# Two-layer hybrid token mixer on one core: where the attention keys of the first head, and the Fourier weights, are put and who loads them

## The chip, the core and the metric

The kernel runs on one core of a Trainium2 chip. The metric is the time of one execution on the device in microseconds. Each kernel is run several times; the median of the runs is the time that counts. A profiled execution gives the trace, whose times count from the start of its span.

## What is computed

Two layers work on 2048 latent tokens and 256 context tokens of width 1024, all in float32. Each layer normalises its input, projects it, sends the parts to four branches, multiplies each by a gate and projects the whole back:

```python
h  = _rmsnorm(x, g) * (1 + scale) + shift
hp = h @ w_in                                   # 1024 -> q, kv, rope, conv, fourier, sgu, gate
attn = _block_attention(q, k_all, v_all)        # 4 heads, 64 + 32 (rope) deep, 2304 keys
conv = _conv_module(hp[..., CONV_OFF:FOUR_OFF], p)
mixed = jnp.fft.fft2(fg, axes=(1, 3), norm="ortho").real      # over tokens and 64 channels
four = mixed @ p["w_fourier"] + p["b_fourier"]
sgu  = _spatial_gating(hp[..., SGU_OFF:GATE_OFF], p)
y = concatenate([attn, conv, four, sgu]) * silu(hp[..., GATE_OFF:]) @ p["w_out"]
x = x + gate * y
```

The context stream goes through the same in the first layer; in the second only its keys and values are needed. The attention's softmax is over all 2304 keys.

## The kernel before

**Tiling.** Tokens and channels are cut into tiles of 128 partitions. Every float32 matmul of weight is written as three matmuls on halves of higher and lower bits (`mm3`, lines 286 to 288): high by high, high by low, low by high. ScalarE rounds a tile to its high half (`split`, L277), VectorE subtracts to get the low half (L278).

**Projection ("phase A").** Per layer, three superblocks of up to 768 tokens are projected. The weights come in blocks of 256 to 384 columns, each by four loads `wst<-winA/B/C` on SyncE's queue into two staging buffers `wst` (`load_w`, L467), and are split into a ring that holds seven loads of a 256-column weight. In the third superblock the weights come in the order f (Fourier input), c0, c1 (convolution) and so on. After the first weight, the Fourier branch is started (`fourier`); its steps are put between the projection's matmuls. It loads its weights `wf` on GpSimd's queue (L805) into a tile `fst` of the Fourier pool, loads its input `fx` back from memory on SyncE's queue (L812), multiplies wf by a cosine matrix on TensorE (L824), and folds fx on GpSimd and VectorE; the folded halves fh, fl and the products wch, wcl are multiplied in a PSUM bank `hold`. Its results go out as `four<-fx` (L925) and `four<-fb` (L961) on SyncE's queue.

**Attention.** After phase A its pool is closed and a pool `K0` is opened at the same addresses. Head 0's and head 1's keys, `k0h`, `k0l`, `k1h`, `k1l`, are 96 rows by 2304 tokens, loaded in three pieces of 512, 768 and 1024 tokens, each by two loads (64 rows of `kh`, 32 rope rows of `krh`). Query tiles `qh`, `ql` cover 256 tokens by three loads each. Then come `v` and the convolution's blocks `cac` (L1464), all of them stored by phase A in memory before. A job is 256 queries for two heads; a tile of 128 queries of one head has four score banks of 512 keys and one of 256. VectorE takes maxima over the banks (L1005), and ScalarE takes exponentials of all five (`e<-s`, L1014) after the last. TensorE transposes them (L1035) and multiplies by v (L1028). The second job in layer 0 is the context's (T), which has one bank of 256 keys per tile. The convolution's tail goes beside: cac is transposed on TensorE (L1484), normalised on VectorE to yn, and transposed back (L1495). A first job may use eight PSUM banks (s five, t two, o one).

**Order and waits.** A scheduler sets each engine's order of instructions; an engine's queue is worked off in order. A tile at an address waits for the last use of the tiles that lay there before. In the pool of phase A the addresses run: `wst`, `m`, the layer's tiles (`uk`, `uq`, `ws`, `bs`), `junk`, `sq`, and then the ring, whose pool lies behind. Head 0's keys, at the front of `K0` behind the q tiles, thus lie over tiles of which `wst` and the ring are used until the last projection; head 1's lie over the ring too.

Who loads: q of the first job for both heads and head 0's keys on GpSimd's queue, head 1's keys, q of the second job, v and cac on SyncE's.

## Time and profile before

| | us |
|---|---|
| median of three runs | 2961.28 |
| lowest, highest | 2960.53, 2970.81 |
| profiled execution | 2965.82 |
| its span | 2963.8 |
| TensorE busy | 2829.0 |
| VectorE busy | 1956.1 |
| ScalarE busy | 1206.9 |
| GpSimd busy | 569.2 |

The profiled execution has 2.0 us outside its span. An engine's busy time leaves out DMA issues. A time line lists instructions with their start, length and, in brackets, the idle time ahead with what ended it. The view of waits adds these idle times up. A view of windows gives each engine's busy time in a stretch, and the clock that was granted to TensorE as a share of full speed: 0.5 is its lower level of 1.2 GHz, 1.0 the upper of 2.4 GHz. A list of DMA issues gives sizes and the median time from issue to landing.

### The profile page before, as it was taken

The numbers are of one execution on the slowest core, as the hardware profiler recorded it, in microseconds if no ns is written. First come the engines' busy times: TensorE is split into PE (matmuls) and PEld (weight loads), VectorE is DVE, ScalarE is ACT, GpSimd is POOL, SyncE is SP. The second block draws the span as 40 slices with busy tenths as digits, with TensorE's granted clock in tenths as the row PEclk, the third lists the DMA queues.
The fourth block names the chain that finished last, engine by engine and source line by source line (L and its number), as shares of the span: only waits on it lengthen the run. The fifth ranks groups of instructions, "written<-read, shape, count | busy, mean of one in ns | idle before, by whom it ended". The sixth has DMA issues, their size and how long they took to land. (4 is left out here: it accounts for less than half of the span.)

```text
span 2963.8 us, 50552 instructions
## 1 busy us (share of the span) xinstructions
PE 2829.0 (95%) x18434; PEld 2429.3 (82%) x18434; DVE 1956.1 (66%) x4301; ACT 1206.9 (41%) x3228; POOL 569.2 (19%) x951
## 2 busy tenths in 40 slices
PE   6999999999699999999999999999979999999998
PEld 4889999899567777769998899998767777776998
DVE  5578488485377777654553695894827777775554
ACT  3432343433344454543322343343425455554432
POOL 2301311421211111112322212113321110011210
PEclk8999999999799999999999999999989999999999
DMA  7465343433521010016543443444453101000653
GB/s 244 139 194 177 107 132 106 161 123 117 163 56 29 29 48 25 21 30 207 182 153 117 157 158 105 137 136 139 148 164 93 33 22 45 18 28 15 187 155 110
DMA packets 221849, 326.75 MB, mean 110 GB/s; under 512 B 33456, under 2 KB 152752, under 8 KB 220832
## 3 DMA queue, kind: packets, MB, share of 16 engines
q1 hardware_dynamic: 191392, 240.66, 26.9%
q0 software_dynamic: 29776, 82.83, 8.3%
q8 instruction: 145, 2.38, 0.3%
q14 instruction: 104, 0.85, 0.1%
q10 hardware_dynamic: 432, 0.04, 0.0%
HBM read 232.30 MB, written 91.10 MB: 109 GB/s over the span
## 5 line engine op out<-in xcount | busy, mean ns | idle before, releaser
L1005 DVE TENSOR_REDUCE st<-s 128x1 f32<-128x512 f32 (+1 forms) x636 | 384.9, 631 | 184.4 <-PE s L288 182.6
L1014 ACT ACTIVATE e<-s,st 128x512 f32<-128x512 f32 (+1 forms) x636 | 399.4, 646 | 236.9 <-DVE st L1009 228.3
L286 PE MATMUL mm<-hh,ring 128*128 128x384 f32 (+1 forms) x1408 | 491.4, 349 | 0.0
L287 PE MATMUL mm<-hl,ring 128*128 128x384 f32 (+1 forms) x1408 | 484.7, 344 | 0.0
L288 PE MATMUL mm<-hh,ring 128*128 128x384 f32 (+1 forms) x1408 | 484.1, 344 | 0.0
L1451 DVE SCALAR_TENSOR_TENSOR acc<-win,c_cw,acc 128x384 f32<-128x384 f32 (+5 forms) x780 | 428.4, 572 | 7.4
L1035 PE MATMUL t<-ident,e 128*128 128x128 f32 x2320 | 341.8, 278 | 3.5 <-DVE et L1038 1.9
L1028 PE MATMUL o<-et,v 128*64 128x256 f32 x2320 | 343.7, 392 | 0.0
L1035 PEld LDWEIGHTS t<-ident,e 128*128 128x128 f32 x2320 | 259.7, 141 | 94.9 <-issue 43.7
L1038 DVE COPY et<-t 128x512 f32<-128x512 f32 x377 | 257.9, 686 | 92.1 <-PE t L1035 86.1
L286 PE MATMUL mm<-yh,woh 128*128 128x256 f32 x1040 | 297.2, 286 | 5.2 <-DVE xn L1223 3.7
L288 PE MATMUL mm<-yh,wol 128*128 128x256 f32 x1040 | 293.9, 283 | 0.2 <-DVE wol L278 0.2
L287 PE MATMUL mm<-yl,woh 128*128 128x256 f32 x1040 | 293.8, 282 | 0.1
L286 PEld LDWEIGHTS mm<-hh,ring 128*128 128x128 f32 x1408 | 267.8, 190 | 19.4 <-issue 9.5
L277 ACT CAST ring<-wst 128x256 fp32r<-128x256 f32 (+2 forms) x480 | 184.1, 418 | 240.2 <-DMA wst<-winC 125.4
L287 PEld LDWEIGHTS mm<-hl,ring 128*128 128x128 f32 x1408 | 267.9, 190 | 5.9
L288 PEld LDWEIGHTS mm<-hh,ring 128*128 128x128 f32 x1408 | 267.3, 190 | 5.8
L278 DVE TENSOR_TENSOR ring<-wst,ring 128x256 fp32r<-128x256 f32 (+2 forms) x480 | 201.2, 451 | 74.6 <-ACT ring L277 60.1
L1040 ACT COPY et<-t 128x512 f32<-128x512 f32 x203 | 119.1, 588 | 317.8 <-PE t L1035 317.6
L1028 PEld LDWEIGHTS o<-et,v 128*64 128x64 f32 x2320 | 153.1, 136 | 99.0 <-issue 51.9
L286 PEld LDWEIGHTS mm<-yh,woh 128*128 128x128 f32 x1040 | 198.4, 191 | 6.9 <-DVE xn L1223 4.3
L287 PEld LDWEIGHTS mm<-yl,woh 128*128 128x128 f32 x1040 | 198.3, 191 | 0.4 <-DVE yl L278 0.4
(319 smaller groups left out, 5284.8 us busy)
## 6 DMA issues: line engine op xcount, KB each, us to landing
wst<-winC SPq DMA_DIRECT2D x192, 256.0 KB, 3.1
ast<-wada SPq DMA_DIRECT2D x32, 512.0 KB, 4.5
gt<-g SPq DMA_DIRECT2D x102, 128.0 KB, 3.0
g<-co POOLq DMA_DIRECT2D x60, 192.0 KB, 2.2
wst<-winB SPq DMA_DIRECT2D x24, 384.0 KB, 3.4
x<-xn POOLq DMA_DIRECT2D x72, 128.0 KB, 2.8
ast<-wada SPq DMA_DIRECT2D x8, 1024.0 KB, 9.6
fst<-ft SPq DMA_DIRECT2D x32, 256.0 KB, 3.2
```

What stands on the lines that cost most here:

```text
L277: a = self.nc.scalar.copy(out=hi, in_=src)
L278: b = self.nc.vector.tensor_tensor(lo, src, hi.bitcast(F32), op=ALU.subtract)
L286: mm(out, lhsT=lh, rhs=rh, start=start and i == 0, stop=False)
L287: mm(out, lhsT=lh, rhs=rl, start=False, stop=False)
L288: self.last = mm(out, lhsT=ll, rhs=rh, start=False, stop=stop and i == n - 1)
L1005: self.red = nc.vector.reduce_max(mx[:, i:i + 1], ps[:, :w], axis=AX.X)
L1014: nc.scalar.activation(out=e, in_=ps, func=AF.Exp, bias=nb[:, 0:1], accum_out=sm[:, i:i + 1])
L1028: nc.tensor.matmul(job.o[64 * q:64 * q + 64, 0:256], lhsT=vt[:, g, 64 * h:64 * h + 64], rhs=et[:, 256 * q:256 * q + 256], start=kt == 0, s ...
L1035: nc.tensor.transpose(ps[:, j * P:(j + 1) * P], job.es[j][kt], self.ident)
L1038: nc.vector.tensor_copy(et, ps)
L1040: nc.scalar.copy(out=et, in_=ps)
L1451: eng.scalar_tensor_tensor(ac, win[:, t:t + w], v["cw"][:, l, c, t:t + 1], ac, op0=ALU.mult, op1=ALU.add)
```

## The change

`phase_a_open` now takes the layer's tiles, `m`, `sq` and `junk` from the pool before the first staging tile, so that these lie in front and `wst` behind them, next to the ring. `K0` takes head 0's keys first, then q, then head 1's keys: head 0's keys and the first q now lie over the layer's tiles, `m`, `sq` and `junk`, and no longer over `wst` and the ring; head 1's keys lie over `wst` and the ring.

All loads of the first two jobs go on SyncE's queue in the order of their use: q of head 0, keys of head 0, q of head 1, keys of head 1, q of the second job, v. The Fourier weights go through a staging tile `wst`, loaded on SyncE's queue right after the weight f, and are read from there by TensorE; their tile in the Fourier pool is gone. The number of loads is the same.

```diff
     def phase_a_open(self, l, lp):
 
+        self.sp = lp
+        self.ltiles = self.layer_tiles(lp)
+        self.m = [self.t(lp, f"m{c}", [P, SBW]) for c in range(2)]
+        self.sq(), self.junk()
         self.ringx = self.pool(f"ring{l}", "left")
...
                 if ci == 0 and i == 2:
+                    wf = self.t(lp, "wst", [P, 768], bufs=2)[:, :512].rearrange("p (a b) -> p a b", b=256)
+                    self.nc.sync.dma_start(out=wf, in_=A["wf"][l])
                     while self.dq:
                         self.tick()
...
-        wf = T_("fst", [P, 512], bufs=2).rearrange("p (a b) -> p a b", b=256)
-        nc.gpsimd.dma_start(out=wf, in_=A["wf"][l])
...
+    def load_k(self, S, kk, h):
+
+        for a, b in ((0, 512), (512, 1280), (1280, NTOK)):
+            s = slice(a, b)
+            for part, k in zip("hl", kk):
+                self.nc.sync.dma_start(out=k[0:64, s].bitcast(F32), in_=S["k" + part][64 * h:64 * h + 64, s])
+                self.nc.sync.dma_start(out=k[64:96, s].bitcast(F32), in_=S["kr" + part][:, s])
...
-                    q0 = [self.load_q(S, k0p, q, 0, nc.gpsimd) for q in range(2)]
-                    keys = self.load_k(S, k0p, 0)
-                    q1 = [self.load_q(S, k0p, q, 256 if last else T, nc.sync) for q in range(2)]
+
+                    keys = [[self.t(k0p, f"k0{part}", [96, NTOK], F32R) for part in "hl"]]
+                    q0 = [self.load_q(S, k0p, 0, 0)]
+                    self.load_k(S, keys[0], 0)
+                    q0.append(self.load_q(S, k0p, 1, 0))
+                    keys.append([self.t(k0p, f"k1{part}", [96, NTOK], F32R) for part in "hl"])
+                    self.load_k(S, keys[1], 1)
+                    q1 = [self.load_q(S, k0p, q, 256 if last else T) for q in range(2)]
                     nc.sync.dma_start(out=vt, in_=S["v"][:, :, :])
```

The order of instructions shows where this lands. SyncE's queue at the end of phase A in layer 0, before; a name ahead of the arrow is the tile written, behind it the source, and the brackets hold what the instruction waits for (PE is TensorE, DMAHW a load on SyncE's own queue, DMASW one on GpSimd's):

```order
L961 DMA four_110<-fb_7604 128x256 [waits DVE_49]
L961 DMA four_110<-fb_7672 128x256 [waits DMAHW6_49,DVE_49]
L975 DMA k1h_7829<-kh_94 64x512 [waits DMAHW7_49,PE_49,Activation_49]
L976 DMA k1h_7829<-krh_98 32x512 [waits DMAHW0_49]
L975 DMA k1l_7830<-kl_95 64x512 [waits DMAHW1_49]
```

The same place in the changed kernel:

```order
L963 DMA four_110<-fb_7606 128x256 [waits DVE_49]
L963 DMA four_110<-fb_7674 128x256 [waits DMAHW7_49,DVE_49]
L988 DMA qh_7803<-qh_96 64x256 [waits DMAHW0_49]
L991 DMA qh_7803<-qrh_100 16x256 [waits DMAHW1_49]
...
L972 DMA k0h_7801<-kh_94 64x512 [waits DMAHW6_49]
L973 DMA k0h_7801<-krh_98 32x512 [waits DMAHW7_49]
...
L991 DMA ql_7827<-qrl_101 16x256 [waits DMAHW7_49]
L972 DMA k1h_7831<-kh_94 64x512 [waits DMAHW0_49,PE_49,Activation_49]
```

The wait for TensorE stood ahead of the first key load; now 24 loads stand ahead of it.

SyncE's queue in the third superblock of layer 1, before, from the second load of c0 to the Fourier input (`fst<-ft` are the Fourier tables):

```order
L467 DMA wst_22810<-winC 128x512 [waits DMAHW3_49,DMAHW1_49,DVE_49]
L467 DMA wst_22816<-winC 128x512 [waits DMAHW2_49,DVE_49]
L467 DMA wst_22822<-winC 128x512 [waits DMAHW3_49,DVE_49]
L467 DMA wst_22971<-winC 128x512 [waits DMAHW4_49,DVE_49,Activation_49]
L467 DMA wst_22977<-winC 128x512 [waits DMAHW5_49,DVE_49]
L467 DMA wst_22983<-winC 128x512 [waits DMAHW6_49,DVE_49]
L467 DMA wst_22989<-winC 128x512 [waits DMAHW7_49,DVE_49]
L467 DMA wst_23136<-winC 128x512 [waits DMAHW0_49,DVE_49]
L812 DMA fx_22861<-f_17362 128x2048 [waits DMASW2_49,DMASW4_49,DMASW1_49,PE_49]
```

The same place in the changed kernel, from the Fourier weights on:

```order
L776 DMA wst_22794<-wf 128x512 [waits DMAHW1_49,DVE_49]
L467 DMA wst_22810<-winC 128x512 [waits DMAHW4_49,DMAHW2_49,DVE_49]
L467 DMA wst_22816<-winC 128x512 [waits DMAHW4_49,DVE_49]
L467 DMA wst_22822<-winC 128x512 [waits DMAHW5_49,DVE_49]
L467 DMA wst_22828<-winC 128x512 [waits DMAHW6_49,DVE_49]
L467 DMA wst_22975<-winC 128x512 [waits DMAHW7_49,DVE_49]
L467 DMA wst_22981<-winC 128x512 [waits DMAHW0_49,DVE_49]
L814 DMA fx_22865<-f_17364 128x2048 [waits DMASW3_49,DMASW1_49,PE_49]
L860 DMA fst_22965<-ft 128x512 [waits DMAHW3_49,PE_49]
L467 DMA wst_22987<-winC 128x512 [waits PE_49]
```

The four loads of c0 and two of c1 now pass through the one buffer that wf leaves free; the third of c1 waits for TensorE's last use of wf.

TensorE in layer 0, from the last scores of the first job to the first cac, before:

```order
L288 MATMUL s_8013<-k1h_7829,ql_7811 128x256
L286 MATMUL s_8076<-k0h_7815,qh_7843 128x256 [waits DMAHW4_49,DMAHW5_49,DMAHW3_49,Activation_49]
L287 MATMUL s_8076<-k0l_7816,qh_7843 128x256
L288 MATMUL s_8076<-k0h_7815,ql_7847 128x256 [waits DMAHW7_49,DMAHW6_49,DMAHW0_49]
L1484 MATMUL t_8092<-ident,cac_7872 128x128 [waits DMAHW0_49,Activation_49]
```

And in the changed kernel (the twelve matmuls of the T job's four tiles, of which the first and the last are shown):

```order
L288 MATMUL s_8015<-k1h_7831,ql_7827 128x256
L286 MATMUL s_8078<-k0h_7801,qh_7845 128x256 [waits DMAHW5_49,DMAHW6_49,DMAHW4_49,Activation_49]
...
L286 MATMUL s_8182<-k1h_7831,qh_7853 128x256 [waits Activation_49]
L287 MATMUL s_8182<-k1l_7832,qh_7853 128x256
L288 MATMUL s_8182<-k1h_7831,ql_7857 128x256
L1492 MATMUL t_8094<-ident,cac_7874 128x128 [waits DMAHW1_49]
```

One T tile's scores stood ahead of cac; now all four do.

## Rows read from the trace of the kernel before

**Rows 1.** Busy time of TensorE, share of the span and instructions (page, part 1).

```profile
PE 2829.0 (95%) x18434; PEld 2429.3 (82%) x18434; DVE 1956.1 (66%) x4301; ACT 1206.9 (41%) x3228; POOL 569.2 (19%) x951
```

**Rows 2.** TensorE's waits: us in total, times, longest in us.

```profile
PE s L286 <- DMA k0l<-krl: 27.5, 2, 14.1
...
PE hold L824 <- DMA fst<-wf: 10.8, 2, 6.3
...
PE mm L286 <- ACT ring L277: 4.6, 2, 3.8
...
PE hold L286 <- ACT fh L277: 1.9, 1, 1.9
```

**Rows 3.** Time line, TensorE, attention's start in layer 0: start, length, instruction, idle before.

```profile
764.21 0.77 PE L286 MATMUL s<-k0h,qh 96*128 96x512 f32 x1 [13.47 <-DMA k0l<-krl]
...
792.14 0.40 PE L288 MATMUL s<-k1h,ql 96*128 96x512 f32 x1
792.38 0.28 PE L286 MATMUL s<-k1h,qh 96*128 96x256 f32 x1
...
792.62 0.28 PE L288 MATMUL s<-k1h,ql 96*128 96x256 f32 x1
...
793.57 0.44 PE L1484 MATMUL t<-ident,cac 128*128 128x128 f32 x2
...
796.97 0.41 PE L1495 MATMUL t<-ident,yn 128*128 128x128 f32 x2 [0.32 <-DVE yn L1491]
```

**Rows 4.** Time line, TensorE, attention's start in layer 1.

```profile
2207.99 0.77 PE L286 MATMUL s<-k0h,qh 96*128 96x512 f32 x1 [14.05 <-DMA k0l<-krl]
...
2230.89 0.38 PE L1484 MATMUL t<-ident,cac 128*128 128x128 f32 x2
```

**Rows 5.** Window: busy time by engine, then TensorE's granted clock, DMA share, GB/s.

```profile
740.00:780.00 40.00, 19.76 (x82) 16.69 (x82) 1.88 (x3) 2.76 (x4) 13.76 (x27) 0.68 0.69 193
```

**Rows 6.** Time line, SyncE's queue, end of phase A in layer 0.

```profile
733.20 5.99 SPq L961 DMA_DIRECT2D four<-fb  x2
750.81 0.52 SPq L975 DMA_DIRECT2D k1h<-kh  x1
...
765.94 0.42 SPq L1311 DMA_DIRECT2D v<-v  x1
```

**Rows 7.** Time line, GpSimd, head 0's first and last key load in layer 0.

```profile
757.65 0.54 POOL L975 DMA_DIRECT2D k0h<-kh  x1
...
768.64 0.49 POOL L976 DMA_DIRECT2D k0l<-krl  x1
```

**Rows 8.** Time line, TensorE, products of the Fourier weights, both layers.

```profile
593.15 2.05 PE L824 MATMUL hold<-fst,c_cd 128*128 128x256 f32 x4 [4.42 <-DMA fst<-wf]
...
600.35 1.02 PE L824 MATMUL hold<-fst,c_cd 128*128 128x256 f32 x4
...
2079.16 3.57 PE L824 MATMUL hold<-fst,c_cd 128*128 128x256 f32 x8 [6.34 <-DMA fst<-wf]
```

**Rows 9.** DMA issues of the whole run (page, part 6): count, size, median us to landing.

```profile
wst<-winC SPq DMA_DIRECT2D x192, 256.0 KB, 3.1
```

**Rows 10.** DMA issues between 2060 and 2078 us, layer 1's third superblock.

```profile
wst<-winC SPq DMA_DIRECT2D x4, 256.0 KB, 4.3
fx<-f SPq DMA_DIRECT2D x1, 1024.0 KB, 9.7
```

**Rows 11.** Page, part 5: exponentials, count, busy us, mean ns, idle before.

```profile
L1014 ACT ACTIVATE e<-s,st 128x512 f32<-128x512 f32 (+1 forms) x636 | 399.4, 646 | 236.9 <-DVE st L1009 228.3
```

**Rows 12.** DMA issues between 745 and 780 us, attention's start in layer 0.

```profile
v<-v SPq DMA_DIRECT2D x1, 2304.0 KB, 11.3
...
cac<-dw SPq DMA_DIRECT2D x2, 128.0 KB, 12.0
```

**Rows 13.** Time line, SyncE's queue, layer 1: Fourier input, and the last Fourier stores.

```profile
2063.37 0.34 SPq L812 DMA_DIRECT2D fx<-f  x1
...
2179.09 3.19 SPq L925 DMA_DIRECT2D four<-fx  x2
```

More of the change, by code (lines that the diff above doesn't have):

```diff
@@ L737, in phase_a @@
         A = self.A
-        self.sp = lp
-        M = [self.t(lp, f"m{c}", [P, SBW]) for c in range(2)]
-        W, tiles = {}, self.layer_tiles(lp)
+        M, W, tiles = self.m, {}, self.ltiles
         self.later(1, lambda: W.update(self.layer_weights(l, lp, tiles)))
@@ L1092, in load @@
         def load(i):
-            return [self.load_q(S, qpool, 2 * pr + q, qs[i], self.nc.sync) for q in range(2)]
+            return [self.load_q(S, qpool, 2 * pr + q, qs[i]) for q in range(2)]
         ahead = list(first or [])
@@ L1324, in build @@
                         self.avq, self.avw, self.ep = [], None, k1p
-                        self.attention(l, S, p, vt, k0p, 0, keys, side, lambda: kn.extend(self.load_k(S, k1p, 1)), [q0, q1])
+                        self.attention(l, S, p, vt, k0p, 0, keys, side, lambda: kn.extend(self.load_keys(S, k1p, 1)), [q0, q1])
                         k0.__exit__(None, None, None)
```

23 lines of the change are left out of this document (8 added, 15 removed).

## The prediction

> **What bounds the kernel now.** I read the busy table first: TensorE works 2829.0 us, 95% of the span [rows 1], so only what shortens TensorE's holes is worth anything. The view of TensorE's waits says where they are [rows 2]. At the start of attention, scores wait for head 0's keys, 27.5 us in two waits. In the third superblock of the projection the Fourier weights are waited for, 10.8 us in two waits. Two smaller entries matter below: 4.6 us for a projection weight, 1.9 us for a Fourier operand. The third view is the time line around each hole.
>
> Attention, layer 0: the first score, at 764.21, stands 13.47 us after the last projection, which thus ended at 750.74 [rows 3]. The first job's scores end at 792.9. The transposition of cac (the convolution's blocks) is at 793.57, that of yn (the same, normalised) at 796.97, 3.4 us behind. In layer 1 the hole is 14.05 us before 2207.99, and cac is transposed at 2230.89 [rows 4]. TensorE is slow besides: the granted clock is 0.68 between 740 and 780 us, a mean of its half and full levels [rows 5].
>
> The loads tell why. SyncE ends its Fourier stores at 739.2 (733.20 + 5.99), then stands until 750.81, when head 1's first key load goes out [rows 6], just after the last projection. GpSimd issues q first and reaches head 0's keys at 757.65; their last load goes out at 768.64 [rows 7]. What is used first is loaded last, and everything waits for the projection's end.
>
> The Fourier weights are loaded by GpSimd after the previous weight's matmuls, and TensorE waits 4.42 us for them in layer 0, 6.34 us in layer 1 [rows 8].
>
> **The change part by part.**
>
> *Keys of head 0, layer 0.* In the changed order SyncE issues, right behind the two Fourier stores, 6 q loads, head 0's 12 key loads and 6 q loads of head 1. Only then, ahead of head 1's keys, comes a wait for the last projection. Pace: 24 issues took 15.13 us between 750.81 and 765.94, 0.63 us each, among crowded transfers [rows 6]. At that pace the first 18 loads, from 739.2, are out by 750.5. Weight loads of 256 KB, as large as the largest key load, landed in 3.1 us on the mean and 4.3 in a crowd [rows 9, 10]. So the first of three key pieces is there before 750.7 and the last about 754.5, when it is needed. The 13.47 us go, the second wait for keys too, and the slow clock behind them.
>
> What is late next is ScalarE. A query tile of a head has five banks of exponentials at 0.646 us [rows 11], 3.2 us, and the fourth tile's last scores need banks that the third's exponentials free. Estimate: the first two tiles are interleaved, 24 matmuls of 0.23 us and 6 of 0.12 [rows 3], 6.3 us; then three times 3.2 us of exponentials, and 1 to 2 us for the last banks. From 750.7 the scores end at 767.6 to 769, against 792.9.
>
> Then comes a bound that the change leaves in its old place: v and cac. Before, they went out at 765.94 and just after [rows 6], and took 11.3 and 12.0 us [rows 12]. Now they stand behind 48 loads on SyncE instead of 24. Of these, 24 move ahead: from 739.2 at 0.52 us each (what the first issue takes by itself [rows 6], with the transfers not yet crowded) they end at 751.7; head 1's 12 key loads and 12 q loads follow at 0.58 to 0.63, which puts v at 765.6 to 767. With head 0's keys out of the way I take 9 to 11 us for cac's landing: 775 to 778.5. TensorE's list now has four T scores ahead of cac where one stood before; these fill until some 772. So a **new wait for cac** of some 5 us appears, and yn follows 3.4 us later, at 778.5 to 782. Against 796.97 that gains 15 to 18.5 us. **I take 17**; the range has 14 (head 1's keys late) to 20.5 (cac there at 773).
>
> *Layer 1.* The same; its Fourier stores on SyncE end at 2182.3 (2179.09 + 3.19) [rows 13], 11.6 us ahead of the last projection's end at 2193.94, just as in layer 0. By layer 0's pace the scores end 17 to 18 us after that, near 2211.5, where cac's transposition, behind them in the old list, stood at 2230.89. Now nine score banks of the next job stand between, so v and cac, some 24 to 27 us after the last projection, are waited for 0 to 3 us. The gain is 13 to 19; **I take 16.5**.
>
> *Fourier weights, layer 0.* The load moves to SyncE, right behind the previous weight's loads, and lands long before its use. The 4.42 us go. The four matmuls behind the wait took 2.05 us, four later ones 1.02 [rows 8], so 1.0 us of slow clock goes, and some 0.6 of the projection behind. That is 6 us. The price: the tile is one of two staging buffers, and until its last use all weight loads go one by one through the other. A hop is landing plus two casts and subtractions, some 4.2 us (3.1 and 1.1). A weight has four, 17 us, and its 96 matmuls of 384 columns last 16.6 (0.17 each, in proportion); the ring holds seven loads besides. I allow 0.5: **gain 5.5** (4 to 6.5).
>
> *Fourier weights, layer 1.* Here a weight lasts only 48 matmuls of 0.23 us, 11.3 us, so four hops don't fit; the ring's stock must bridge. And the Fourier input fx stands behind six hops in SyncE's list: it went out at 2063.37 [rows 13] when two buffers served; with one, the six hops take 25 us, 5 to 6 more than they did, so I put it at 2069 (an estimate). It took 9.7 us to land then [rows 10], so it is there at 2075 to 2078.5, and sums, split and cast add 3 to 4 (an estimate). TensorE, early by 6.34 us, would want the result at about 2077.5 and gets it at 2078.5 to 2082. The second half of fx follows the first, and TensorE waited 1.9 us for it already [rows 2]. So of 7.5 us (6.34 and the slow clock) about 3 come back as a **wait for fh**. **Gain 4.5** (0 to 7.5).
>
> *Start of layer 1's projection.* The first staging tile now lies over output weights that are used up a product earlier, so its load can leave some 2 us sooner into the 3.8 us wait of [rows 2]. **Gain 1.5** (0 to 2.2).
>
> *The queues.* GpSimd loses 50 issues of about 0.5 us, and nobody waits for it there. SyncE gains 50; its pace of 0.63 us is in the sums.
> The Trainium skill has a rule against this: "Perfetto Trace Analysis", section DMA Optimizations, says that where generating descriptors is the bottleneck, balancing DMAs over the engines that can issue them may help. By that rule 48 loads on one queue are worse than on two; no run yet has them side by side with the tiles free. What it would make of the time is rival 2.
>
> **The sum.** 17 + 16.5 + 5.5 + 4.5 + 1.5 = 45 us. The profiled execution took 2965.82 us, of which 2.0 lie outside its span; less 45 it is 2920.8. It was 0.15% above the median, 2961.28, so the median to expect is **2916 us**, a ratio of 0.985. The terms' lower ends add to 31 us, the upper ends to 55.7.
>
> **The rivals.**
>
> 1. *The one staging buffer eats the Fourier gain.* If a hop takes 5.0 us instead of 4.2 (the 4.3 us landing of the crowded stretch), fourteen hops, eight in layer 0 and six in layer 1, cost 11 us and the 10 us of both layers go. Attention's 33.5 and the 1.5 remain: 2926.
>
> 2. *One queue is the bound of the first job.* For it: all 48 loads stand in one line. Against it: SyncE's pace was 0.63 us among crowded transfers. At GpSimd's pace, 11 issues in 11.0 us [rows 7], the 18 early loads end at 757, head 1's keys at 775, and the scores some 5 us after the last landed, near 784 instead of 792.9; v leaves at 787 and holds back the rest. Attention gains 9 to 10 us a layer, and 31 us remain in all: 2930.
>
> 3. *The tiles aren't free early.* If one of the first loads waits for something as late as the last projection, SyncE stands there with all behind it. Loads then start at 750.8 as now, though in order of use: first scores at 758, head 1's keys out by 770, v at 777, cac there at 788, yn at 792 instead of 797. That gains 3 to 5 us a layer, with the weights 18 to 20 at best and 9 if rival 1 holds too: 2942 to 2952. Against it: in the changed order no wait for TensorE stands ahead of head 0's loads.
>
> 4. *Slower than before.* The one staging buffer again, in a crowd: its loads land beside fx and its stores. With 8.5 us of landing a hop is 9.6 us and fourteen are 134 us, against some 50 us of matmuls that they feed and 29 in the ring's stock: 55 us lost, more than attention's 35. That would be 2981. It decides from a landing of 7.0 us; the crowded stretch shows 4.3.
>
> **How the numbers follow.** Forecast 0.64, rival 1 0.11, rival 2 0.13, rival 3 0.08, rival 4 0.04. The predicted time is the forecast's. The range takes in rivals 1 and 2 and the ends of the terms: 2902 to 2940. A measurement of this kernel can tell about 0.5%, 14.8 us, from no change; the border is 2946.5. Forecast, rivals 1 and 2 and a part of 3 are faster, 0.89; the rest of 3 is the same, 0.07; slower has 0.04.
>
> **What would show it.** Right: scores begin within 1 us of the last projection in both layers at full clock, no wait for wf is left, and the largest new TensorE waits are cac's in layer 0 (up to 5 us) and fh's in layer 1. Rival 1: waits of mm for ring in the third superblock. Rival 2: SyncE's issues over 0.8 us apart after 740, and waits for k1. Rival 3: SyncE stands until 750 as now. I am wrong as a whole if these waits are gone and the time isn't shorter: another engine, ScalarE most likely, would then have set attention's pace all along.

## The result, and the profile of the changed kernel

The changed kernel takes 2932.3 us (median of four runs, 2923.2 to 2941.0) against 2960.9 for the kernel before, a ratio of 0.9897 with a 95% interval of 0.9859 to 0.9935. Run again later, beside other experiments (e5), it gave 2925.0 us and 0.9887 (0.9864 to 0.991). It is faster by 29 to 37 us. That lies inside the range of the prediction, 2902 to 2940, but short of the 45 us that the terms add up to.

The view of TensorE's waits in the changed kernel (us in total, times, longest) answers [rows 2]:

```profile
...
PE s L286 <- ACT e L1017: 12.8, 10, 2.0
...
PE mm L286 <- ACT ring L277: 4.3, 3, 2.0
PE o L286 <- ACT e L1017: 3.9, 2, 1.9
PE hold L286 <- ACT fh L277: 3.4, 1, 3.4
...
PE mm L288 <- DVE ring L278: 1.7, 2, 1.1
PE t L1492 <- DMA cac<-dw: 1.3, 2, 0.9
```

The 27.5 us for keys and the 10.8 us for the Fourier weights are gone. Behind a load at the program's start (14.4 us, 15.6 before) the largest entry is now one that the kernel before had as 4.9 us: scores that wait for a bank which ScalarE has not emptied yet (s and o together 16.7 us).

The time line of SyncE's queue at the end of the projection of layer 0 (start, length, instruction) answers [rows 6]: the loads go out while the projection still runs, in order of use, 0.57 us apart on the mean (48 issues in 27.3 us).

```profile
736.49 0.51 SPq L988 DMA_DIRECT2D qh<-qh  x1
...
739.72 0.45 SPq L972 DMA_DIRECT2D k0h<-kh  x1
...
750.40 0.45 SPq L972 DMA_DIRECT2D k1h<-kh  x1
...
756.50 0.58 SPq L973 DMA_DIRECT2D k1l<-krl  x1
...
763.80 0.42 SPq L1319 DMA_DIRECT2D v<-v  x1
764.26 0.92 SPq L1472 DMA_DIRECT2D cac<-dw  x2
```

TensorE's time line of the same place answers [rows 3]. The first score follows the last projection without a gap; then come four waits for banks, cac's transposition and yn's.

```profile
747.65 0.34 PE L288 MATMUL mm<-hh,ring 128*128 128x384 f32 x1
747.82 0.40 PE L286 MATMUL s<-k0h,qh 96*128 96x512 f32 x1
...
754.70 0.50 PE L286 MATMUL s<-k0h,qh 96*128 96x512 f32 x1 [1.55 <-ACT e L1017]
...
759.17 0.50 PE L286 MATMUL o<-k1h,qh 96*128 96x512 f32 x1 [1.94 <-ACT e L1017]
...
766.74 0.50 PE L286 MATMUL s<-k1h,qh 96*128 96x512 f32 x1 [1.47 <-ACT e L1017]
...
770.55 0.58 PE L286 MATMUL s<-k0h,qh 96*128 96x256 f32 x1 [1.46 <-ACT e L1017]
...
773.35 0.47 PE L1492 MATMUL t<-ident,cac 128*128 128x128 f32 x1 [0.45 <-DMA cac<-dw]
...
776.49 0.66 PE L1503 MATMUL t<-ident,yn 128*128 128x128 f32 x2 [0.75 <-DVE st L1012]
```

Windows of that stretch (busy time of TensorE, weight loads, VectorE, ScalarE, GpSimd; then the granted clock, DMA share and GB/s) show the clock beside the waits: it is full until 760, through the first two waits for banks, then it falls to a mixture of its two levels and from 770 to 780 to the lower one.

```profile
750.00:755.00 5.00, 3.45 (x17) 2.59 (x16) 3.64 (x8) 1.14 (x3) 0.00 (x0) 1.00 0.66 200
755.00:760.00 5.00, 3.05 (x14) 2.00 (x13) 2.50 (x6) 5.00 (x18) 0.00 (x0) 1.00 0.81 232
760.00:765.00 5.00, 5.00 (x18) 3.95 (x16) 1.77 (x3) 0.24 (x2) 0.00 (x0) 0.66 0.38 89
...
770.00:775.00 5.00, 4.00 (x16) 3.63 (x17) 1.13 (x5) 2.82 (x11) 0.00 (x0) 0.50 0.53 188
775.00:780.00 5.00, 4.25 (x14) 2.97 (x14) 3.98 (x14) 1.64 (x5) 3.26 (x5) 0.50 0.39 107
```

Where the gain arises and where it goes is read from **shifts**: the start of a matmul less the start of the same matmul in the kernel before (same operands, same place in the count). What a stretch adds to the shift is what it won or lost. The table has this for all kernels of this case, by marks near 550, 735, 880, 1530, 1690, 2010, 2160, 2330 and 2930 us of the kernel before, worked out from the time lines of TensorE; minus is time won. The first 550 us are left out: they differ by 1.4 to 10.6 us from run to run, also in e1, which changes nothing there. Two runs of the changed kernel agree within 1.4 us in each stretch. Other kernels differ by more where their edit changes nothing: e2, e8 and e9 leave attention as it is in the changed kernel and have -13.4 to -16.3 and -3.6 to -5.5 us in its two stretches, and between 880 and 1530, which no kernel here touches, the table goes from -3.7 to 3.4.

| kernel | Fourier, L0 | attention's start, L0 | 880 to 1530 | start of L1 | 1690 to 2010 | Fourier, L1 | attention's start, L1 | rest | from 550 on |
|---|---|---|---|---|---|---|---|---|---|
| predicted | -5.5 | -17 | 0 | -1.5 | 0 | -4.5 | -16.5 | 0 | -45 |
| changed kernel | -0.9 | -14.0 | -1.6 | -5.8 | 1.4 | -3.5 | -6.7 | 1.3 | -29.8 |
| e5, the same again | -1.8 | -14.1 | -2.4 | -4.5 | 0.6 | -2.7 | -7.1 | 1.3 | -30.6 |
| e1, weights alone | -0.1 | -2.0 | -0.4 | -0.2 | -0.1 | -2.5 | -0.7 | 0.2 | -5.6 |
| e2, keys alone | 0.3 | -13.5 | -1.3 | -2.0 | -0.2 | 1.0 | -4.1 | 1.0 | -18.9 |
| e3, tile 4 behind tile 3 | -0.3 | -15.0 | 2.2 | -6.2 | 0.5 | -4.1 | -8.8 | 0.3 | -31.4 |
| e4, cac and v sooner | -1.8 | -14.7 | 3.3 | -7.2 | 1.1 | -3.5 | -9.0 | -0.3 | -32.2 |
| e6, both mends | -0.7 | -15.4 | -2.2 | -3.5 | 0.9 | -3.5 | -10.3 | 0.3 | -34.4 |
| e7, two queues | -0.1 | -9.3 | 1.1 | -1.9 | -1.0 | -2.9 | -3.9 | 0.4 | -17.7 |
| e8, weights' own tile | 4.9 | -13.4 | -2.0 | -6.0 | 7.0 | -6.0 | -5.5 | 1.2 | -20.0 |
| e9, one half of fx | -2.4 | -16.3 | -0.3 | -5.7 | 0.5 | -4.7 | -3.6 | -0.2 | -32.7 |
| e10, half exponentials | -0.3 | -16.6 | -3.2 | -3.3 | 2.4 | -3.5 | -4.8 | 1.2 | -28.0 |
| e11, a third of the scores | -0.5 | -14.7 | -3.7 | -6.4 | 1.8 | -1.9 | -8.8 | -0.5 | -34.8 |
| e12, three mends | -6.8 | -13.3 | 3.3 | -6.1 | 0.2 | -5.9 | -10.5 | -0.2 | -39.3 |

A difference of 3 us in one stretch, and of 7 between 880 and 1530, is thus about what these runs scatter. Against that two terms are missing in the main: nearly all of the Fourier gain of layer 0, and 10 us of attention's start in layer 1.

### The profile page after: what moved, and what is told of

It is laid out like the page before. It is cut to its first block, busy times and chain, and to the rows that moved or that the text cites. A ratio compares the mean times of both kernels' runs of the same rounds, so it can differ in the third digit from the quotient of the medians.

```text
span 2931.3 us, 50512 instructions
## 1 busy us (share of the span) xinstructions
PE 2826.8 (96%) x18434; PEld 2425.8 (83%) x18434; DVE 1958.5 (67%) x4301; ACT 1207.0 (41%) x3228; POOL 549.8 (19%) x901
## 5 line engine op out<-in xcount | busy, mean ns | idle before, releaser
L1038 PEld LDWEIGHTS t<-ident,e 128*128 128x128 f32 x2320 | 261.5, 142 | 96.4 <-issue 42.4
```

The costliest lines, as they stand in the source:

```text
L1038: nc.tensor.transpose(ps[:, j * P:(j + 1) * P], job.es[j][kt], self.ident)
```

## The experiments

### The two halves of the change apart

**e1** puts only the move of the Fourier weights into the kernel before, **e2** leaves only that move out of the changed kernel:

```diff
-        wf = T_("fst", [P, 512], bufs=2).rearrange("p (a b) -> p a b", b=256)
-        nc.gpsimd.dma_start(out=wf, in_=A["wf"][l])
+                    wf = self.t(lp, "wst", [P, 768], bufs=2)[:, :512].rearrange("p (a b) -> p a b", b=256)
+                    self.nc.sync.dma_start(out=wf, in_=A["wf"][l])
```

> The kernel before with only the Fourier weights moved to a staging tile on SyncE; keys and their queues as before. The prediction's terms say 10 us less (5.5 in layer 0, 4.5 in layer 1). The changed kernel's trace, read by how far each matmul moved, says the 6.7 us won at the wait in layer 0 are given back by 725 us to about 1, and that layer 1 keeps about 3.5: 4 to 5 us less, 2955 to 2958 us. If the staging buffer cost nothing and something else gave the time back, it would be the full 10, 2951 us.

> The changed kernel without the move of the Fourier weights, which are loaded by GpSimd into the Fourier pool as before; key tiles, their queue and their order as in the changed kernel. The prediction's terms say 35 us less (17, 16.5 and 1.5). The changed kernel's trace says 14 and 7 for the two attention starts and up to 6 at the start of layer 1: 25 to 28 us less, 2933 to 2936 us.

Measured on one chip: e1 2947.3 us, 0.997 (0.9957 to 0.9983) of the kernel before; e2 2930.3 us, 0.9923 (0.9903 to 0.9944). The two differences to 2956.1, 8.8 and 25.8 us, add up to 34.6, about what the whole change gives. Keys alone carry most of it. e1's 8.8 us are more than the 4 to 5 expected; its trace has 5.6 from 550 us on, and no run says where the rest is. By the shifts only 2.6 arise in the two Fourier stretches. In layer 0 the hole for the weights goes, and nothing is left of that 150 us later.

### Where the Fourier gain goes

The time lines of the changed kernel show it. The weights' products start without a wait:

```profile
586.78 1.02 PE L826 MATMUL hold<-wst,c_cd 128*128 128x256 f32 x4
```

TensorE is 6.7 us ahead there. But the Fourier input fx has one buffer for its two halves, and the second half is loaded when GpSimd has summed the first. GpSimd, SyncE and VectorE, in this order:

```profile
587.97 3.26 POOL L815 TENSOR_TENSOR fe<-fx 128x1023 f32<-128x1023 f32 x1 [2.02 <-DMA fx<-f]
...
597.84 3.41 POOL L815 TENSOR_TENSOR fe<-fx 128x1023 f32<-128x1023 f32 x1 [4.03 <-DMA fx<-f]
```

```profile
592.18 0.33 SPq L814 DMA_DIRECT2D fx<-f  x1
```

```profile
597.79 1.23 DVE L816 TENSOR_TENSOR fo<-fx 128x1023 f32<-128x1023 f32 x1 [2.93 <-DMA fx<-f]
598.96 2.58 DVE L278 TENSOR_TENSOR ring<-wst,ring 128x256 fp32r<-128x256 f32 x1
...
602.07 0.41 DVE L278 TENSOR_TENSOR ring<-wst,ring 128x256 fp32r<-128x256 f32 x1
```

VectorE waits 2.93 us for the second half, and behind it in its list stands the subtraction that makes a projection weight ready. That one takes 2.58 us beside GpSimd's second sum, and 0.41 when the sum is over. TensorE then waits for the weight, and its clock dips (time line, and two windows):

```profile
601.60 0.44 PE L288 MATMUL mm<-hh,ring 128*128 128x384 f32 x1 [1.14 <-DVE ring L278]
```

```profile
600.00:604.00 4.00, 2.65 (x14) 1.81 (x13) 3.60 (x6) 1.61 (x4) 2.53 (x4) 0.99 0.22 71
604.00:608.00 4.00, 4.00 (x22) 4.00 (x21) 3.89 (x9) 0.71 (x2) 1.55 (x2) 0.58 0.47 154
```

In e5, the same kernel again, that wait is 0.47 us, and one for another of VectorE's products (ftl) is 1.55. So the hole had covered something else that was late: in the kernel before, VectorE stood idle for 3.45 us up to 602.03, beside most of GpSimd's second sum. Three kernels test what is late. **e8** gives the Fourier weights a tile of their own, paid for with a shorter weight ring, so that both staging buffers serve the projection again:

```diff
-RING = 7168
+RING = 6656
...
-                    wf = self.t(lp, "wst", [P, 768], bufs=2)[:, :512].rearrange("p (a b) -> p a b", b=256)
+                    wf = self.t(lp, "wft", [P, 512]).rearrange("p (a b) -> p a b", b=256)
```

> The changed kernel with a tile of its own for the Fourier weights, so that both staging buffers serve the projection's weights again; its 2 kB come out of the weight ring (6656 elements instead of 7168), since there is no other room. If the one staging buffer gives back the gain of the Fourier hole in layer 0 (won 6.7 us at the hole, 1.0 left at the end of the superblock): shift over 575 to 725 us goes from -1 to between -4 and -6, over layer 1's Fourier stretch from -3.5 to between -5 and -7.5, the waits for ring in the third superblock (3.0 us) go, and the time is 4 to 8 us under the changed kernel. If something else gives it back (the ring's order of use, VectorE's queue): the shift stays within 1.5 us of -1. If the smaller ring costs more than the buffer gives: waits for ring elsewhere in the projection, and a time 0 to 6 us above.

It took 2937.7 us, 0.9926 (0.9903 to 0.995), 12.7 us above the changed kernel on the same chip. The gain at the hole is given back all the same, 4.9 us beyond it. VectorE waits for the second half of fx even longer, and TensorE for the weight behind:

```profile
596.10 1.23 DVE L816 TENSOR_TENSOR fo<-fx 128x1023 f32<-128x1023 f32 x1 [5.08 <-DMA fx<-f]
597.25 2.58 DVE L278 TENSOR_TENSOR ring<-wst,ring 128x256 fp32r<-128x256 f32 x1
```

```profile
599.88 0.69 PE L288 MATMUL mm<-hh,ring 128*128 128x384 f32 x1 [5.23 <-DVE ring L278]
```

None of the sizes expected came. The kernel is confounded by its shorter ring (7.0 us more are lost between 1690 and 2010, where no Fourier step runs), and by GpSimd: its first sum begins 12.9 us after fx was sent for, behind the load altr in its list, where it was 6.2 in the changed kernel; no run says why that load went out so late. Two staging buffers did not save the gain; by itself e8 does not say that one is enough.

**e9** leaves out the load of fx's second half; all sums stay:

```diff
-            f = T_("fx", [P, T])
-            nc.sync.dma_start(out=f, in_=S["f"][c * P:(c + 1) * P, 0:T])
+            if c == 0:
+                f = T_("fx", [P, T])
+                nc.sync.dma_start(out=f, in_=S["f"][c * P:(c + 1) * P, 0:T])
```

> The changed kernel without the second half's load of the Fourier input: its sums are taken from the first half's tile again (the load and its wait are left out, all sums stay). Theory F (the hole for the weights had hidden the second half of fx, which waits for GpSimd's sum of the first half in the one fx buffer, and behind whose sum VectorE's ring weights stand): in layer 0 VectorE no longer waits 2.9 us for fx, TensorE's wait for ring at the end of that weight goes, and the shift over 575 to 725 us goes from -1.0 to -1.8 (two runs of the changed kernel) to between -4.5 and -6.5; in layer 1 the wait for fh, 3.4 us, falls under 1 and the shift of that stretch goes from -3 to between -5.5 and -7. Rival (the one staging buffer, as the prediction had it): the shifts stay within 1.2 us of the changed kernel's.

2923.5 us in one execution beside 2956.9. The stretches are -2.4 and -4.7 us, better than the changed kernel's by 0.6 to 2.0, but short of the expectation: the load is a part of it, not the whole. In layer 0 TensorE's wait for the weight is still 0.63 us, and in layer 1 its wait for fh 1.09, with 1.42 for fl behind it. GpSimd's sums were still there and slowed VectorE: its two differences fo took 4.56 us where 2.4 are usual, fg 2.09 where 0.69 is, and two ring subtractions 1.83 where 0.75 are usual, these last beside a later step of GpSimd (the fold of fe into fg) that e12 leaves to GpSimd too.

**e12** takes those sums from GpSimd, and keeps the load, the one staging buffer and the long ring. It has the two mends of attention besides, of which the next part tells:

```diff
-            nc.gpsimd.tensor_tensor(fe[:, c, 1:N2], f[:, 1:N2], f[:, N - 1:N2:-1], op=ALU.add)
+            nc.vector.tensor_tensor(fe[:, c, 1:N2], f[:, 1:N2], f[:, N - 1:N2:-1], op=ALU.add)
...
-            nc.gpsimd.tensor_copy(fe[:, c, 0:1], f[:, 0:1])
-            nc.gpsimd.tensor_copy(fe[:, c, N2:N2 + 1], f[:, N2:N2 + 1])
+            nc.vector.tensor_copy(fe[:, c, 0:1], f[:, 0:1])
+            nc.vector.tensor_copy(fe[:, c, N2:N2 + 1], f[:, N2:N2 + 1])
```

> Three mends at once, nothing left out: the fourth query tile queued behind the third, cac and v loaded ahead of the second job's q, and the Fourier input's even sums made by VectorE instead of GpSimd, so that the one fx buffer comes free some 3 us sooner (a VectorE sum of this size took 1.23 us, GpSimd's 3.3 with 1.0 of copies behind it) and no GpSimd sum runs beside VectorE's subtractions (a ring subtraction took 2.58 us beside one, 0.43 else). If fx's buffer and GpSimd's sum hold the Fourier stretches: layer 1's wait for fh (3.4 us) falls under 1, that stretch shifts by 5 to 7 us instead of 3, layer 0's by 3 to 5 instead of 1 to 1.8, and the time is 4 to 8 us under the changed kernel with the two attention mends (0.9876 of the kernel before): 0.985 to 0.9865. If VectorE's own list is what holds them: the 2.5 us of sums that it takes over show as later ring weights, the stretches shift as before within 1 us, and the time stays at 0.987 to 0.990.

2917.3 us (2913.5 to 2919.9), 0.9861 (0.9842 to 0.9879), the fastest kernel of this case by its median and by its shift from 550 us on. The intervals overlap that of the changed kernel, so the step from it is told by the traces, 8.7 to 9.5 us. The Fourier stretches have -6.8 and -5.9 us, where e6, which differs from e12 in these sums alone, has -0.7 and -3.5: in layer 0 the whole gain at the hole is kept, more than the 3 to 5 us expected. The wait for fh in layer 1 is 1.18 us, not under 1. VectorE does both sums in 2.4 us, fg takes 0.69 where it took 1.84 beside GpSimd's first sum, and no weight is late (time line of VectorE, then the wait for fh that is left in layer 1):

```profile
591.02 1.22 DVE L815 TENSOR_TENSOR fe<-fx 128x1023 f32<-128x1023 f32 x1
592.16 1.22 DVE L816 TENSOR_TENSOR fo<-fx 128x1023 f32<-128x1023 f32 x1
...
593.42 0.69 DVE L836 TENSOR_TENSOR fg<-fo 128x511 f32<-128x511 f32 x1
...
594.48 0.42 DVE L278 TENSOR_TENSOR ring<-wst,ring 128x256 fp32r<-128x256 f32 x1
```

```profile
2061.93 0.39 PE L286 MATMUL hold<-wch,fh 128*128 128x256 f32 x1 [1.18 <-ACT fh L277]
```

The staging buffer is thus acquitted; GpSimd's sums are what gave the gain back. Of the 8.5 us by which e12 is ahead of e6 in the Fourier stretches, 4.9 are left in the sum from 550 us on; 5.5 are lost between 880 and 1530, which is within the scatter there. e12 frees fx sooner and spares VectorE at once; which of the two counts more is not separated, but e9, which does away with the wait for fx alone, got the smaller part.

### The first jobs of attention

The next table is read from the time lines of TensorE: from a layer's first score to the end of the first job's scores, and to the transposition of cac and of yn (us).

| kernel | scores, L0 | cac, L0 | yn, L0 | scores, L1 | cac, L1 | yn, L1 |
|---|---|---|---|---|---|---|
| before | 28.7 | 29.4 | 32.8 | 22.1 | 22.9 | 35.3 |
| changed | 20.4 | 25.5 | 28.7 | 20.6 | 33.1 | 40.5 |
| e3 | 20.2 | 25.0 | 28.1 | 20.3 | 31.1 | 38.4 |
| e4 | 20.8 | 21.2 | 32.4 | 22.1 | 22.4 | 38.9 |
| e6 | 20.7 | 20.5 | 31.7 | 21.4 | 21.3 | 37.6 |
| e7 | 32.4 | 32.6 | 36.6 | 31.4 | 31.9 | 44.6 |
| e10 | 23.6 | 27.4 | 30.5 | 21.1 | 34.6 | 42.4 |
| e11 | 16.4 | 25.2 | 28.4 | 15.9 | 31.0 | 38.4 |

In layer 1 the scores of the first job took 22.1 us before, some 18 of them at half clock, and take 20.6 now, though the clock starts full. Before, TensorE was slow and had one wait of 0.84 us for a bank. Now it outruns the chain of maximum, exponential and freed bank, has waits of 1.5, 1.9 and 1.5 us, and the clock falls behind the second. ScalarE by itself isn't the bound: between the second and the third query tile's exponentials it stands idle, in layer 0 (time line of ScalarE) for 5.67 us.

```profile
765.91 0.69 ACT L1017 ACTIVATE e<-s,st 128x512 f32<-128x512 f32 x1 [5.67 <-issue]
```

The third tile's exponentials wait for the last of its five maxima, and its scores stand among the fourth tile's.

Two windows of 43 us from the first score in layer 1 on, of the kernel before and of the changed one:

```profile
2207.00:2250.00 43.00, 40.60 (x172) 29.02 (x173) 28.94 (x60) 21.63 (x65) 4.94 (x9) 0.78 0.72 201
```

```profile
2167.00:2210.00 43.00, 35.10 (x150) 25.41 (x149) 23.87 (x51) 22.00 (x63) 3.45 (x6) 0.84 0.69 204
```

TensorE is busy 35.1 us of 43 where it was 40.6, at 0.84 instead of 0.78 of its clock: 29.5 against 31.7 us of full-speed work. The hole of 14.05 us is gone, and 7.3 us come back behind it. At the end of the first job's scores the changed kernel is ahead by 21.9 us in layer 0 and 15.7 in layer 1 (e5: 21.3 and 15.7); behind them, up to the marks, 7.9 and 9.0 are lost (7.2 and 8.7). In layer 1 the scores of the second job, which wait for banks too, stand ahead of cac's transposition and the exponentials':

```profile
2190.50 0.80 PE L286 MATMUL s<-k0h,qh 96*128 96x512 f32 x1 [0.82 <-ACT e L1017]
...
2197.00 0.50 PE L286 MATMUL s<-k0h,qh 96*128 96x512 f32 x1 [1.96 <-ACT e L1017]
...
2200.68 0.42 PE L1492 MATMUL t<-ident,cac 128*128 128x128 f32 x1
```

**e3** keeps the fourth query tile's scores behind the third's in TensorE's list; in the changed kernel its scores, which wait for banks, stand among them. **e4** loads cac and v ahead of the second job's q, and with that cac's and e's transpositions move ahead of the second job's scores in layer 1. **e6** has both.

```diff
+            if self.behind is not None:
+                with self.tc.issue_after(self.behind):
+                    self.mm3(*args)
...
+                self.behind = self.last.ins if first and i == 0 and j == 3 else None
```

```diff
-                    q1 = [self.load_q(S, k0p, q, 256 if last else T) for q in range(2)]
-                    nc.sync.dma_start(out=vt, in_=S["v"][:, :, :])
...
+                        nc.sync.dma_start(out=vt, in_=S["v"][:, :, :])
+                        q1 = [self.load_q(S, k0p, q, 256 if last else T) for q in range(2)]
```

> The changed kernel, with the scores of the first job's fourth tile (head 1, second 128 queries) queued on TensorE behind the last score of the third tile; nothing else is asked for. Theory of the order: the changed list has score matmuls of the fourth tile, which wait for banks, ahead of the third tile's last matmuls, and so the third tile's exponentials start 12.1 us after the first instead of 9.0; with the order restored they start at about 9 and 3 us a layer come back, some 6 in all (2926 us). Theory of ScalarE's pace: the exponentials are the bound whatever the order, less than 1.5 us in all. Theory of the clock: holes before the third tile remain, so the granted clock still falls to 0.5 between 768 and 781 us, and less than 2 us come back.

> The changed kernel with cac and v loaded ahead of the second job's q on SyncE. TensorE's list then has the transpositions of cac and of the first exponentials between the first job's scores and the second job's, where the changed kernel has up to nine score banks that wait for exponentials. Theory of the order: in layer 1 the second job's two tiles of exponentials come 6 us apart as before instead of 11, and 4 to 5 us come back there, 1 to 3 in layer 0: 5 to 8 us less than the changed kernel (2924 to 2927 us). Theory of ScalarE's pace: nothing comes back. Theory of the loads: q of the second job lands behind the 2.3 MB of v, its scores wait for it, and some microseconds are lost instead.

> The changed kernel once more, unaltered, so that the three kernels beside it have it on their own chip. Expected 0.988 to 0.991 of the kernel before, as it had (0.9897), 2922 to 2932 us. In the trace, shift of equal matmuls against the kernel before: -1 over the Fourier transform of layer 0, -14 over attention's start of layer 0, -3.5 over the Fourier transform of layer 1, -6.7 over attention's start of layer 1, each within 1.5 us; first exponential tiles of the first job 0, 3.1, 12.1, 15.2 us after the first. If these stretches differ by more than 3 us from one chip to the other, my reading of the first trace by stretches is too fine.

> Both mends of the first job together: the fourth query tile's scores queued behind the third's, and cac and v loaded ahead of the second job's q. Theory A (what was given back in the first two jobs is the order, of TensorE's list and of the loads): the two gains of the single mends (some 3 us by their traces each, over both layers) add up, the time is 5 to 7 us under the changed kernel's in this job, 0.9875 or less of the kernel before; layer 1's attention shift goes from -6.7 to -11 or more. Theory B (ScalarE's chain of maximum, exponential and freed bank, with TensorE at half clock between, sets the pace whatever the order): 0 to 3 us under the changed kernel, within its interval.

Times: e3 2923.4 us, 0.9894 (0.988 to 0.9909); e4 2925.1, 0.9902 (0.9887 to 0.9917); on the other chip e5, the changed kernel again, 2925.0; e6 2925.2, 0.9876 (0.9846 to 0.9907). None stands apart from the changed kernel by its time. By the stretches, the order is worth nothing that can be told in layer 0 (1 us), and about 2 to 3 us in layer 1: -8.8, -9.0 and -10.3, and -10.5 in e12, against -6.7 and -7.1. Each is little more than the scatter, but all four are ahead of the five runs with the changed kernel's attention (-3.6 to -7.1). e4, e6 and e12 lose 4.6 to 5.2 us behind the first job in layer 1, where the changed kernel loses 9.0 and 8.7; the scores of the first job end 0.5 to 1.4 us later in them. e3 and e4 lose 2.2 and 3.3 us between 880 and 1530: at 1375 to 1378 us stands a wait of 2.2 and 2.7 us for VectorE's xn that the changed kernel's first trace does not have; e6 has two of 0.7 there, and no run says why. My expectations, 6 us for e3, 5 to 8 for e4 and 5 to 7 for e6 under the changed kernel, were too high.

What the order lays bare is the load of head 1's keys. In e3 the third tile's exponentials start 1.6 us sooner in layer 0 and 1.0 in layer 1, the fourth's as before; and where the third tile's scores go first, they wait for k1, 2.4 us in all in e3 and 5.6 in e6. The longest such wait of e6, in layer 1:

```profile
2176.93 0.77 PE L286 MATMUL s<-k1h,qh 96*128 96x512 f32 x1 [2.95 <-DMA k1h<-krh]
```

**e10** leaves out half of each 512-wide exponential of the first job (the maxima read one half twice, at 0.69 us as before), **e11** two of the three products of each of its scores:

```diff
...
-            nc.scalar.activation(out=e, in_=ps, func=AF.Exp, bias=nb[:, 0:1], accum_out=sm[:, i:i + 1])
+            h = w // 2 if job.half and w == 512 else w
+            nc.scalar.activation(out=e[:, :h], in_=ps[:, :h], func=AF.Exp, bias=nb[:, 0:1], accum_out=sm[:, i:i + 1])
```

```diff
-            self.mm3(ps[:, :w], [(qq[0][:, qs], qq[1][:, qs], kk[0][:, a:a + w], kk[1][:, a:a + w])])
+            if job.short:
+                nc.tensor.matmul(ps[:, :w], lhsT=qq[0][:, qs], rhs=kk[0][:, a:a + w], start=True, stop=True)
+            else:
+                self.mm3(ps[:, :w], [(qq[0][:, qs], qq[1][:, qs], kk[0][:, a:a + w], kk[1][:, a:a + w])])
...
```

> The changed kernel with half of each 512-wide exponential left out in the first job of each layer (the other half is read twice by the transpositions); maxima, scores and loads stay. ScalarE has some 0.28 us less for each of 16 banks, 4.5 us. Theory S (the wait for freed banks sets the pace of the first job): the three waits of scores for exponentials there (1.6, 1.9, 1.5 us) fall to under 0.8 each, the first job's scores end 3 to 5 us sooner behind their start than 20.3 us, and attention's start shifts by 2.5 to 4.5 us more than -14 in layer 0 and -7 in layer 1. Theory O (the list's order and TensorE's own half clock): under 1.5 us in each layer.

> The changed kernel with two of the three products of each score left out in the first job of each layer, 40 of 60 matmuls, 8.3 us at full clock and more at half; exponentials, maxima, loads and list order stay. If TensorE's own work at its lowered clock sets the first job's length: its scores end 8 to 11 us sooner behind their start than 20.3 us. If the chain of maxima, exponentials, freed banks and key loads does: under 4 us sooner, with waits for exponentials or k1 in place of the matmuls, and the granted clock at half level there.

One execution of each: e10 2931.6 us, e11 2928.5, the kernel before beside them 2956.9. e11 is the clearer. 40 of 60 score matmuls are gone, and the scores end only 4.0 and 4.7 us sooner, just outside the "under 4" expected of the chain and far from the 8 to 11 expected of TensorE's own work. There are 18 us of waits for exponentials in the whole run, and 1.2 and 0.4 us for k1h in the first jobs. In layer 0 cac and yn stand where they stood, since cac's load has become the wait:

```profile
773.94 0.48 PE L1496 MATMUL t<-ident,cac 128*128 128x128 f32 x1 [3.73 <-DMA cac<-dw]
...
777.09 0.66 PE L1507 MATMUL t<-ident,yn 128*128 128x128 f32 x2 [0.75 <-DVE st L1015]
```

The stretch is -14.7 us against -14.0, in layer 1 -8.8 against -6.7: 8.3 us of score work less in each layer, and 0.7 and 2.1 us gained. TensorE's own work alone does not set the first job; about half of what it saves reaches the end of the scores, and little of that the end of the stretch. e10 failed to show ScalarE as the bound: its scores end later than the changed kernel's, by 3.2 and 0.5 us, and its stretches, -16.6 and -4.8, lie within the scatter. Its exponentials took 0.47 us instead of 0.69, 3.5 us less in a first job. Its table load fell into the path (1.28 us, which ran beside the first scores in the changed kernel), so it leaves the price of the exponentials by themselves open. What is shown: neither TensorE's score work, nor the lists' order alone, sets the pace at which the first job's banks turn over; what is left is the chain itself, five maxima, their maximum, five exponentials, over eight banks, and the loads: k1's, once the order is right, and cac's and v's behind. No run doubles or halves that chain as a whole, so its part stays argued, not shown.

### One queue or two

**e7** puts head 1's keys and first q on GpSimd's queue:

```diff
...
-                    q0.append(self.load_q(S, k0p, 1, 0))
+                    q0.append(self.load_q(S, k0p, 1, 0, nc.gpsimd))
...
-                    self.load_k(S, keys[1], 1)
+                    self.load_k(S, keys[1], 1, nc.gpsimd)
```

> The changed kernel with head 1's keys and first q on GpSimd's queue; head 0's stay on SyncE, and so do the second job's q, v and cac, which move up by 18 loads. In TensorE's list the third tile's scores now end ahead of the fourth's, and cac's and e's transpositions stand where they stood in the kernel before. If the one queue is what keeps the first job (rival 2 of the prediction, and the balancing rule of the Trainium skill's Perfetto Trace Analysis): cac lands by 765 instead of 773, yn is transposed by 770, and the time falls by 5 to 10 us against the changed kernel. If order alone counts: 2 to 4 us, as with the order of tiles set by hand. If GpSimd issues at its old pace of 1.0 us (11 issues in 11 us): head 1's last key piece goes out at 762 instead of 756.5, scores wait for k1 some 3 to 5 us a layer, and the time is the changed kernel's or up to 6 us above.

2934.1 us, 0.9914 (0.9891 to 0.9938): 9 us slower than the changed kernel on the same chip, in attention's start 4.7 us in layer 0 and some 3 in layer 1. GpSimd did not issue slowly (0.51 us each, the last 10.2 us after the first score, SyncE's in the changed kernel 8.7 after). The loads landed late: DMA issues between 742 and 775 us, of the changed kernel and of e7 (size, median us to landing), and e7's waits for them:

```profile
k1h<-kh SPq DMA_DIRECT2D x1, 256.0 KB, 4.2
k1l<-kl SPq DMA_DIRECT2D x1, 256.0 KB, 4.3
```

```profile
k1h<-kh POOLq DMA_DIRECT2D x1, 256.0 KB, 12.1
k1l<-kl POOLq DMA_DIRECT2D x1, 256.0 KB, 13.1
```

```profile
PE s L287 <- DMA k1l<-krl: 13.1, 4, 6.6
...
PE s L286 <- DMA k1h<-krh: 8.4, 4, 4.4
```

The second queue let q, v (2304 KB) and cac start beside the keys, and all shared the transfers. The single queue kept the order of use. The Trainium skill's balancing rule ("Perfetto Trace Analysis", DMA Optimizations) is for a bottleneck in generating descriptors; here spreading the loads cost 9 us. Another of its pages, "DMA: Bandwidth & Descriptors", section Issuing engines are not separate DMA queues, says that DMAs of all issuers run on the same engines and interleave, and that more issuers save only the time of issuing. The trace agrees with that page: k1h landed in 4.2 us on one queue and in 12.1 on two.

## Why the prediction was right, and where it was off

**The mechanism was right.** In both layers the first score follows the last projection at once. No wait for wf is left. SyncE's early loads stand where the sum put them (first at 736.49, the sum's 739.2 less the shift of 2.8 there), at 0.57 us on the mean instead of 0.63. The new waits for cac in layer 0 (0.45 and 0.89 us) and for fh in layer 1 (3.4 us) are the two that the prediction named; fx went out at 2047.73, which is 2070.4 in the time of the kernel before, where it had 2069.

**Attention in layer 0, 17 foreseen, 14.0 and 14.1 measured.** yn came 17.7 us sooner (20.5 less the shift of 2.8), as the sum had it. The first job's scores took 20.4 us where the sum had 17 to 18 behind the last projection: it laid the exponentials of the tiles end to end, and ScalarE stood idle for 5.67 us among them. The clock was the other part that failed: it was put at full, and stood at half from 770 to 780 and at 0.81 to 0.86 in parts of the 25 us behind, where the kernel before had it full from 790. The term's lower end, 14, was for late keys of head 1, which were not late: that the measured time is just there is luck.

**Attention in layer 1, 16.5 foreseen, 6.7 and 7.1 measured: the step that failed most.** The sum let the scores end 17 to 18 us after the last projection; they took 20.6. At their end 15.7 us of gain are there (2230.07 before, 2188.18 after, less 26.2). 9.0 of them are lost in the second job. "Nine score banks of the next job stand between" was read as filling; they are scores that wait for banks themselves (0.82 and 1.96 us), in large part at half clock, ahead of the exponentials' transpositions and of cac's, which landed at 2194.7 and was transposed at 2200.68. e4, e6 and e12, which have the transpositions ahead, lose 4.6 to 5.2 us there and end the stretch 1.9 to 3.8 us ahead of the changed kernel. What the rest of the 9.0 is stays open. The "slow clock behind" the hole was counted as going with the hole. It moved: TensorE that outruns the chain has new holes, and in e11 faster scores were followed by longer waits behind the first job (11.5 us lost there instead of 9.0).

**Fourier weights, layer 0, 5.5 foreseen, 0.9 and 1.8 measured.** The gain at the hole was right (6.7 measured, 6 foreseen). What is late next was wrong: the prediction looked at the staging buffer and allowed 0.5, and gave the second half of fx a thought in layer 1 alone. e12 shows that the gain is kept with one buffer when GpSimd makes no sums there. So rival 1 had the right size (its 2926 us is nearly the 2925.0 of e5) with the wrong cause, and only in part: the missing 10 us of layer 1's attention are more. Its hop of 5.0 us does not come out of its own rows either: 4.3 us of landing and 1.1 are 5.4.

**Fourier weights, layer 1, 4.5 foreseen, 3.5 and 2.7 measured**, with the wait for fh at 3.4 instead of 3. **Start of layer 1, 1.5 foreseen, 5.8 and 4.5 measured**; some 2 to 3 of them arise at the projection's first weights, as foreseen. The rest is luck: it arises at one wait of q's projection for VectorE's th, 3.73 us before and 1.26 and 0.94 now, which the prediction did not look at. Keys alone have 2.0 us in the whole stretch and still 3.22 of that wait, weights alone 0.2 and 3.27, and no run says why.

**The total.** That it lies in the range is in part luck. Fourier weights in layer 0 and attention in layer 1 fell below the lower ends of their own terms, by 2 to 3 and by 6 us; the start of layer 1 is above its upper end by 2 to 4, and the range was wide because it took in rivals 1 and 2. The two measured times also hold the first 550 us, where the change does nothing: in the two profiled executions 1.9 and 9.5 us.

**The rivals.** Rival 2 fell as a rival: one queue at 0.57 us made no wait for keys in the changed kernel, and two queues are 9 us slower. Its sign, waits for k1, shows in e3, e6 and e12, where the list asks for head 1's keys sooner. Rival 3 fell, the loads were early. Rival 4 fell, the ring's waits went from 5.5 to 6.9 us in all. That "another engine, ScalarE most likely" holds attention's pace was named as what would make the prediction wrong as a whole; the chain that ScalarE is a part of holds the banks, but its share of what layer 1 lost is argued, not shown, and ScalarE by itself stands idle within it.

## What to carry to other kernels

When a hole is closed, ask what else was late under it: here the weights' hole covered a buffer that another engine released slowly, and moving two sums from GpSimd to VectorE was worth 8.5 us in the Fourier stretches (e12 against e6; 4.9 from 550 us on), the closed holes by themselves 4.4. A TensorE that starts sooner and at full clock does not keep all of that gain when its next work waits for banks: here 21.9 and 15.7 us at the end of the first job became 14.0 and 6.7. Look at what stands in its list behind; with transpositions ahead of waiting scores some 2 to 4 us more were kept in layer 1, and nothing that can be told in layer 0. Loads in order of use on one queue can beat two queues: with a 2304 KB load started beside it, a 256 KB key load landed in 12.1 us instead of 4.2.

## What the runs showed that I had not expected

A two-input VectorE instruction on SBUF that starts behind a two-input GpSimd instruction takes several times its usual time: 2.58 us against 0.41 for a ring subtraction, and in layer 1 2.76 against 0.69 for fg. The subtraction ended at 601.54, 0.3 us after GpSimd's sum; the difference fo, which started just ahead of that sum, took its usual 1.23. The Trainium skill has it ("SBUF — State Buffer", Who interferes with whom: both read through one shared port, and the later one stands still); the rows agree, and the prediction should have used it. In the changed kernel's layer 1:

```profile
2054.70 2.76 DVE L836 TENSOR_TENSOR fg<-fo 128x511 f32<-128x511 f32 x1
```

And taking 40 of 60 matmuls out of a job that TensorE seemed to bound moved the end of its scores by 4.0 and 4.7 us only.
